# Shifted copies of y by quarter of the channels, the layer norm's steps in another order, and a second SiLU for the high part of z

## The chip, the cores and the metric

The kernel runs on one core of one Trainium2 chip. The metric is device time in microseconds (us) for one launch. The engines are named as the profile names them: PE (TensorE matmul) and PEld (its weight loads), DVE (VectorE), ACT (ScalarE), POOL (GpSimd), SP (SyncE, which issues nearly all DMAs here, in order).

## What is computed

A trunk of two layers works on 256 latent tokens and 256 context tokens of 1024 channels in float32. Layer 0 mixes tokens by a Conformer convolution module, layer 1 by retention, and each is followed by a SwiGLU network. Every sub-layer is an RMS norm with a shift, a scale and a gate that come from the condition (`adaln`). The change lies in the convolution module of layer 0, which runs on both sequences (512 tokens together):

```python
def conv_module(h, w1, b1, dw, dw_b, norm_g, w2):
    y = h @ w1 + b1
    a, gt = jnp.split(y, 2, axis=-1)
    y = a * jax.nn.sigmoid(gt)
    y = depthwise_conv(y, dw, width=31) + dw_b     # each channel by itself, along the tokens
    y = jax.nn.silu(layer_norm(y, norm_g))         # over the 1024 channels of a token
    return y @ w2

x = x + g_m * conv_module(modulate(x, norm_mix, sh_m, sc_m), ...)
x = x + g_f * swiglu_ffn(modulate(x, norm_ffn, sh_f, sc_f), ...)
```

The shifts, scales and gates are six vectors of 1024 for each sequence, `silu(c) @ ada_w + ada_b`. Three of them (mixer) are needed around the module, the FFN's shift and scale straight behind it.

## The kernel before

Channels lie on the 128 partitions, in eight blocks (`KC`), and the 512 tokens along the free dimension. Every large product is made of three matmuls (`mm3`) on values split into a rounded high part and a rest: high by high, high by low, low by high, in the type fp32r. The high part is a copy that rounds, the low part a subtraction.

The program is written in a layer that schedules by itself, with a timeline of its own, and sets the semaphores; instructions under `pin` keep the order in which they are written among the pinned ones of their engine. The products of w2 are not pinned, the ada blocks, the norm and the loads are.

For each block of channels the module forms a and g (`pair_half`, `start_products`), then y (`glu`), and the depthwise convolution's 31 taps are shared: 16 taps on PE (`dwconv_pe`), about nine on DVE (`dwconv_dve`), and five or six as ACT products with POOL additions (`dwconv_pool`). `total` adds the three. For PE's share, `bounce_out` writes y to DRAM (`yd`) and `bounce_in` reads it back into `z4`: four planes, one for each quarter of 32 channels, in which the 128 partitions hold the 32 channels of the quarter at four shifts of one token. One matmul (contraction over channel and shift, through the block-diagonal `dg`) then does four taps of 32 channels, and 16 of them make a block's `cv`. Before the change, SP issues `dg` and then four DMAs, one for each shift; each fills 32 partitions in all four planes. Blocks follow each other in a loop of eight steps; the convolution of block c stands two steps behind its y, and the last two blocks come after the loop.

The layer norm's mean and mean square come from matmuls: `stats(ch)` multiplies the block and its square by a column of 1/1024 (`mean32`) and adds up in the accumulator `pst` over all eight blocks. `pst` is copied to SBUF (`srow`), turned by a matmul (`ptk`, tokens on the partitions: tile `stats_t`) for the inverse root, which runs as thirteen small DVE steps on 128 x 4 values, and spread over all partitions for the mean (`mean_bc`, copy `mb`). POOL subtracts `mb` from the eight blocks; `token_row(rn)` spreads the inverse root (`rstd_bc`); then, block by block, DVE multiplies (`z_norm`, tile `zt`), ACT applies the SiLU with the gain (`zs`), DVE rounds the high part (`ah_z`) and subtracts for the low part (`al_z`), and PE multiplies by w2 (tile `w`, two halves n of the columns, four groups t of tokens, eight k).

Beside this, PE computes the vectors of `adaln`, in blocks i of 256 columns: `begin(i)` (16 matmuls, L239), `evict(i)` (ACT, L245), `cols(i)` (four small matmuls, L251) and `finish(i)` (ACT, L258). Blocks 8 to 11 are the mixer's gates, 12 to 19 the FFN's shift and scale. They serve as filling while the norm's chain runs: 8 to 15 stand before z, 16 and 17 in the z loop, 18 and 19 in the first half of w2. `gate_to_rows` turns the gates and sends them through DRAM. Blocks 12 to 15 are loaded into the memory of the module's input h (tags `ah` and `al`, which z takes over later), behind a small POOL memset; 16 and 17 into `z4`'s two buffers, 18 and 19 into others. PSUM has six accumulators (`acc`) and two `aux` tiles; `ADA_AUX` says which ada blocks use `aux`. Memory of the pool `cv` is given to later tiles (`crow`, `rawt`) when the z loop is done with it.

Of the kernel before, what the change touches and what calls it, by code (L numbers as in the profile page):

```python
# [8 lines left out]
F32 = mybir.dt.float32  # L9
F32R = mybir.dt.float32r  # L10
I32 = mybir.dt.int32
# [49 lines left out]
W2_AT = 3  # L61
PACC = 2
ADA_AUX = (16, 17, 18, 19)
ADA_K4 = (8, 9, 18)
# [17 lines left out]
def trunk_kernel(ctx: ExitStack, tc, x_in, ctx_in, cond, small, consts, rope, dist, ada, adas, adat,  # L82
# [406 lines left out]
    def bounce_in(ch, yd):  # L489

        n = GROUPS[ch]
        dg = cv.tile([P, MAXG, 4, 32], F32, tag="dg", name="dg", bufs=2)
        pin(nc.sync.dma_start(dg[:, :n], dwd[:, ch, :n]))
        z4 = cv.tile([P, 4, 2 * YW], F32, tag="z4", name="z4", bufs=Z4)
        w = 2 * YW - 3
        for s in range(4):
            pin(nc.sync.dma_start(z4[32 * s:32 * s + 32, :, 0:w], yd[:, :, s:s + w].rearrange("q c t -> c q t")))
        return z4, dg
# [67 lines left out]
    def stats(ch):  # L566
        for i, src in enumerate((yc[:, ch, :], sqs.pop(ch))):
            q = 2 * (ch % 2) + i
            pin(nc.tensor.matmul(pst[32 * q:32 * q + 32, :], mean32, src, start=(ch < 2), stop=(ch >= KC - 2)))
# [143 lines left out]
    fills = [pA.tile([P, 4096], F32, tag=tag, name=f"raw_fill_{tag}") for tag in ("ah", "al")]  # L713
    pin(nc.gpsimd.memset(fills[0][:, 0:1], 0.0))
    for i in range(12, 16):
        t = fills[(i - 12) // 2][:, 2048 * (i % 2):2048 * (i % 2) + 2048]
        pin(nc.sync.dma_start(t, ada[ADA_PE.index(i)]))
        ada_raws[i] = halves(t)
    w2r[0, 1] = load(w2[0, 1], name="w2_01", also=pin)
    for i in (16, 17):  # L720
        t = cv.tile([P, 4, 2 * YW], F32, tag="z4", name=f"raw_ada{i}", bufs=Z4).rearrange("p q t -> p (q t)")[:, 0:2048]
        pin(nc.sync.dma_start(t, ada[ADA_PE.index(i)]))
        ada_raws[i] = halves(t)
    cols(8)
# [10 lines left out]
    stats(c)  # L735
    cols(10)
    finish(10)
    begin(11)
    cbs[d] = dwconv_pe(d, zs4.pop(d))
    evict(11)  # L740
    cols(11)
    total(d)
    finish(11)
    square(d)
    stats(KC - 1)
    begin(12)
    srow = t2("srow")
    pin(nc.scalar.activation(srow, pst, AF.Copy))
    evict(12)
# [3 lines left out]
    pmd = aux("mean_bc")  # L753
    for q in range(4):
        pin(nc.tensor.matmul(pmd[32 * q:32 * q + 32, :], sel2[:, 0:1].to_broadcast([P, 32]), srow, start=True, stop=True))
    mb = cv.tile([P, 512], F32, tag="sq", name="mb", bufs=2)
    begin(13)
    cols(12)
    pin(nc.scalar.activation(mb, pmd, AF.Copy))
    evict(13)  # L760
    finish(12)
    cols(13)
    finish(13)
    gate_to_rows(0, 0, pin)
    gates = [gate_bc(0, 0, 0, pin), gate_bc(0, 0, 1, pin)]
    ada_raws[18] = ada_load(18, pin)
    ada_raws[19] = ada_load(19, pin)
    begin(14)
    evict(14)
    for ch in range(KC):  # L770
        pin(nc.gpsimd.tensor_tensor(yc[:, ch, :], yc[:, ch, :], mb, op=ALU.subtract))
    st = cv.tile([P, 4, 2], F32, name="st")
    nc.vector.tensor_copy(st.rearrange("p t i -> p (t i)"), ptk[:, 0:8])
    md, vv = st[:, :, 0], st[:, :, 1]
# [9 lines left out]
    mq = cv.tile([P, 4], F32, name="mq")  # L784
    va = cv.tile([P, 4], F32, name="va")
    rn = cv.tile([P, 4], F32, name="rn")
    nc.vector.tensor_tensor(mq, md, md, op=ALU.mult)
    nc.vector.scalar_tensor_tensor(va, vv, EPS, mq, op0=ALU.add, op1=ALU.subtract)

    nh, pt = ptk[:, 8:12], ptk[:, 12:16]  # L790
    nc.vector.tensor_scalar(rn.bitcast(I32), va.bitcast(I32), -0.5, 1597463007.0, op0=ALU.mult, op1=ALU.add)
    nc.vector.tensor_scalar(nh, va, -0.5, None, op0=ALU.mult)
    for i in range(3):
        nc.vector.tensor_tensor(pt, nh, rn, op=ALU.mult)
        nc.vector.tensor_tensor(pt, pt, rn, op=ALU.mult)
# [655 lines left out]
```

## Time and profile before

| what | value |
|---|---|
| median of three runs | 1101.52 us (1101.11 to 1102.01) |
| the profiled execution's own time | 1103.33 us |
| its span in the profile | 1101.2 us |
| mean granted PE clock | 0.991 |
| PE busy | 1069.0 us (97%) |
| DVE, ACT, POOL busy | 700.6, 417.5, 161.6 us |
| data moved | 190.29 MB, mean 173 GB/s |

The span is what the profile covers; the execution's own time has some 2 us around it. A busy PE is not PE at its peak: matmuls overlap, and their ends are modelled. A granted clock below 1.00 in a stretch means that PE ran its matmuls slower there. In a group's row, the name left of the arrow is the tile written; L507 and the like are lines of the kernel above.

### The profile page before, as it was taken

To read this page: it belongs to the slowest core of one execution; us is meant where nothing else is said; L and a number is where in the kernel's file an instruction comes from. 1 tells how busy PE (TensorE), PEld (TensorE's weight loads), DVE (VectorE), ACT (ScalarE), POOL (GpSimd) and SP (SyncE) were. 2 spreads that over 40 slices of the span, in tenths; PEclk is the share of its full clock that TensorE was granted. 3 is DMA by queue.
4 is the path that set the end of the run, shared out by engine and by line. 5 is a ranking of instruction groups with operands and counts; after the bars stand their busy time and mean duration, and the time that the engine had idled before them with its cause. 6 is when DMAs were issued, how large, how long until landed. Compare 5 with 4: busy or idle time off the path is not lost.

```text
span 1101.2 us, 13492 instructions
## 1 busy us (share of the span) xinstructions
PE 1069.0 (97%) x5302; PEld 845.0 (77%) x5302; DVE 700.6 (64%) x1147; ACT 417.5 (38%) x607; POOL 161.6 (15%) x119
## 2 busy tenths in 40 slices
PE   6989998999999999999999999999999989999998
PEld 2766654789888888888888788888888868888886
DVE  3988873757999877545644796366364555555445
ACT  4474463343222122212232564234333454444442
POOL 0077853030000000000000330000000461000000
PEclk8999998999999999999999999999999999999999
DMA  9469778732566576533313342334333344455551
GB/s 372 181 179 264 223 195 348 265 115 99 191 248 249 201 296 234 186 114 116 115 59 132 135 143 106 115 134 155 113 115 115 115 152 155 172 190 191 190 182 49
DMA packets 35185, 190.29 MB, mean 173 GB/s; under 512 B 3953, under 2 KB 4401, under 8 KB 16177
## 3 DMA queue, kind: packets, MB, share of 16 engines
q1 hardware_dynamic: 34688, 187.87, 49.0%
q10 hardware_dynamic: 434, 1.55, 0.4%
q8 instruction: 42, 0.69, 0.3%
q14 instruction: 21, 0.17, 0.0%
HBM read 185.99 MB, written 3.42 MB: 172 GB/s over the span
## 4 chain that ended last, share of the span: by engine, by line
PE 86%; DVE 6%; DMA 4%; ACT 3%; issue 1%; SPq 0%; POOL 0%; ACTq 0%; DVEq 0%
PE u L202 4%; PE fa L201 4%; PE u L200 4%; PE u L201 4%; PE fa L202 4%; PE fb L201 4%; PE fb L202 4%; PE fa L200 4%; PE fb L200 4%; PE v L201 3%; PE v L202 3%; PE v L200 3%; PE dn L201 3%; PE dn L202 3%; PE dn L200 3%; PE cv L507 2%
## 5 line engine op out<-in xcount | busy, mean ns | idle before, releaser
L171 DVE TENSOR_TENSOR wl_gu<-raw_gu,wh_gu 128x1024 fp32r<-128x1024 f32 x76 | 92.2, 1223 | 82.6 <-ACT wh_gu L163 81.7
L163 ACT ACTIVATE wh_gu<-raw_gu 128x1024 fp32r<-128x1024 f32 x84 | 88.0, 1058 | 139.6 <-PE fb L201 52.6
L851 DVE SCALAR_TENSOR_TENSOR junk<-raw_adat,crow 128x1024 f32<-128x1024 f32 x80 | 97.5, 1219 | 0.9
L171 DVE TENSOR_TENSOR wl_dn<-raw_dn,wh_dn 128x1024 fp32r<-128x1024 f32 x38 | 46.5, 1224 | 45.3 <-ACT wh_dn L163 45.0
L200 PE MATMUL fa<-ah_h0f,wh_gu 128*128 128x512 f32 (+1 forms) x192 | 72.0, 376 | 1.0 <-DVE ah_h0f L324 1.0
L201 PE MATMUL fa<-al_h0f,wh_gu 128*128 128x512 f32 (+1 forms) x192 | 72.3, 376 | 0.1
L200 PE MATMUL fb<-ah_h0f,wh_gu 128*128 128x512 f32 (+1 forms) x192 | 72.1, 376 | 0.0
L202 PE MATMUL fa<-ah_h0f,wl_gu 128*128 128x512 f32 (+1 forms) x192 | 72.0, 375 | 0.0
L202 PE MATMUL fb<-ah_h0f,wl_gu 128*128 128x512 f32 (+1 forms) x192 | 72.0, 375 | 0.0
L201 PE MATMUL fb<-al_h0f,wh_gu 128*128 128x512 f32 (+1 forms) x192 | 72.0, 375 | 0.0
L163 ACT ACTIVATE wh_dn<-raw_dn 128x1024 fp32r<-128x1024 f32 x38 | 40.3, 1060 | 80.1 <-PE dn L202 35.5
L200 PE MATMUL u<-wh_gu,ah_h1f 128*128 128x512 f32 x160 | 63.5, 397 | 0.0
L171 POOL TENSOR_TENSOR wl_qk<-raw_qk,wh_qk 128x1024 fp32r<-128x1024 f32 x4 | 9.6, 2401 | 362.8 <-DVE res L355 350.3
L202 PE MATMUL u<-wh_gu,al_h1f 128*128 128x512 f32 x160 | 62.8, 393 | 0.0
L201 PE MATMUL u<-wl_gu,ah_h1f 128*128 128x512 f32 x160 | 62.2, 390 | 0.0
L523 POOL TENSOR_TENSOR pacc<-pacc,pr 128x512 f32<-128x512 f32 x39 | 58.8, 1508 | 17.8 <-ACT pr L522 15.5
L540 DVE SCALAR_TENSOR_TENSOR lacc<-y,sm,lacc 128x512 f32<-128x512 f32 x65 | 49.1, 755 | 2.1
L201 PE MATMUL v<-wl_v,ah_h 128*128 128x512 f32 x128 | 50.4, 393 | 0.0
L202 PE MATMUL v<-wh_v,al_h 128*128 128x512 f32 x128 | 50.1, 391 | 0.0
L200 PE MATMUL dn<-wh_dn,ah_hid 128*128 128x512 f32 x128 | 49.9, 390 | 0.0
L201 PE MATMUL dn<-wl_dn,ah_hid 128*128 128x512 f32 x128 | 49.8, 389 | 0.0
L202 PE MATMUL dn<-wh_dn,al_hid 128*128 128x512 f32 x128 | 49.8, 389 | 0.0
(308 smaller groups left out, 2669.5 us busy)
## 6 DMA issues: line engine op xcount, KB each, us to landing
raw_gu<-in_gu_dram SPq DMA_DIRECT2D x44, 1024.0 KB, 4.8
raw_adat<-in_adat_dram SPq DMA_DIRECT2D x28, 1024.0 KB, 4.9
raw_dn<-in_dn_dram SPq DMA_DIRECT2D x19, 1024.0 KB, 4.8
raw_ada<-in_ada_dram SPq DMA_DIRECT2D x10, 1024.0 KB, 10.8
z<-yd SPq DMA_DIRECT2D x32, 284.5 KB, 4.9
raw_qk<-in_wqk_dram SPq DMA_DIRECT2D x8, 1024.0 KB, 4.7
raw_v<-in_wv_dram SPq DMA_DIRECT2D x8, 1024.0 KB, 4.8
raw_g<-in_wg_dram SPq DMA_DIRECT2D x8, 1024.0 KB, 4.8
```

The lines of the kernel that those rows point to most:

```text
L163: also(nc.scalar.activation(hi[:, :m], raw[:, c:c + m], AF.Copy))
L171: also((eng or nc.vector).tensor_tensor(lo[:, :m], raw[:, c:c + m], hi[:, :m].bitcast(F32), op=ALU.subtract))
L200: also(nc.tensor.matmul(o, a[0], b[0], start=first, stop=False))
L201: also(nc.tensor.matmul(o, a[0], b[1], start=False, stop=False))
L202: also(nc.tensor.matmul(o, a[1], b[0], start=False, stop=last))
L507: pin(nc.tensor.matmul(cb[32 * q:32 * q + 32, :], dg[:, g, q, :], m, start=(g == 0), stop=(g == n - 1)))
L523: pin(nc.gpsimd.tensor_tensor(pacc, pacc, pr, op=ALU.add))
L540: pin(nc.vector.scalar_tensor_tensor(cacc, a, w, cacc, op0=ALU.mult, op1=ALU.add))
L851: pin(nc.vector.scalar_tensor_tensor(junk, raw[:, c, :], 1.0, crow[:, s, :], op0=ALU.mult, op1=ALU.mult, accum_out=mods[l][:, c0 + c, s:s ...
```

## The change

`bounce_in` issues one DMA for each quarter: its source pattern has 32 channels, four shifts of one token and the row, so that each DMA fills one plane on all 128 partitions, now in the order channel, shift (the host lays out `dwd` to match). The DMAs of z4 come before that of `dg`.

In the norm, the sums in `pst` end with the seventh block; `srow` and its transpose no longer hold the eighth. The eighth block and its square are multiplied as stationary operands with one column of `mean32`, which gives sums for each token on the partitions, and DVE adds both (once to SBUF, once to PSUM). The mean is spread by `token_row`, like the inverse root. The small DVE steps work on PSUM columns. All of these are pinned.

The ada blocks are placed anew: 8 to 10 before the last convolution, 11 and 12 and the sums of 13 between there and z, the rest of 13, and 14 and 15, in the z loop, 16 to 19 in the first half of w2. Their loads move: 12 and 13 into `ah` (without the memset), 14 and 15 into `z4`, 18 and 19 into a pool that opens after the z loop. In the z loop, ACT writes z's high part by a SiLU of its own and runs a second one into PSUM, from which the low part is formed.

```diff
@@ -59,9 +59,11 @@
 K4 = 5
 YW = TOK + 2 * PAD
 W2_AT = 3
+W2_ADA = (2, 4, 6, 7)
 PACC = 2
-ADA_AUX = (16, 17, 18, 19)
-ADA_K4 = (8, 9, 18)
+ADA_AUX = (14, 15, 16, 17, 18, 19)
+ADA_K4 = (8, 9, 16)
+ADA_RAWT = (18, 19)
 T2 = 5
 GU_POOL = (0, 1)
 CTX_AT = ((1, 3), (1, 4), (1, 6), (1, 7))
@@ -489,12 +491,13 @@
     def bounce_in(ch, yd):
         n = GROUPS[ch]
+        z4 = cv.tile([P, 4, 2 * YW], F32, tag="z4", name="z4", bufs=Z4)
+        w = 2 * YW - 3
+        for q in range(4):
+            src = yd[q]
+            pin(nc.sync.dma_start(z4[:, q, 0:w], bass.AP(src.tensor, src.offset, [[2 * YW, 32], [1, 4], [1, w]])))
         dg = cv.tile([P, MAXG, 4, 32], F32, tag="dg", name="dg", bufs=2)
         pin(nc.sync.dma_start(dg[:, :n], dwd[:, ch, :n]))
-        z4 = cv.tile([P, 4, 2 * YW], F32, tag="z4", name="z4", bufs=Z4)
-        w = 2 * YW - 3
-        for s in range(4):
-            pin(nc.sync.dma_start(z4[32 * s:32 * s + 32, :, 0:w], yd[:, :, s:s + w].rearrange("q c t -> c q t")))
         return z4, dg
     def dwconv_pe(ch, zd):
@@ -566,7 +569,7 @@
     def stats(ch):
         for i, src in enumerate((yc[:, ch, :], sqs.pop(ch))):
             q = 2 * (ch % 2) + i
-            pin(nc.tensor.matmul(pst[32 * q:32 * q + 32, :], mean32, src, start=(ch < 2), stop=(ch >= KC - 2)))
+            pin(nc.tensor.matmul(pst[32 * q:32 * q + 32, :], mean32, src, start=(ch < 2), stop=(ch >= KC - 3)))
     ys, zs4, cbs = {}, {}, {}
@@ -710,17 +713,19 @@
     total(c)
     dve_taps(d, cut, TAPS)
-    fills = [pA.tile([P, 4096], F32, tag=tag, name=f"raw_fill_{tag}") for tag in ("ah", "al")]
-    pin(nc.gpsimd.memset(fills[0][:, 0:1], 0.0))
-    for i in range(12, 16):
-        t = fills[(i - 12) // 2][:, 2048 * (i % 2):2048 * (i % 2) + 2048]
+    fill = pA.tile([P, 4096], F32, tag="ah", name="raw_fill")
+    for i in (12, 13):
+        t = fill[:, 2048 * (i % 2):2048 * (i % 2) + 2048]
         pin(nc.sync.dma_start(t, ada[ADA_PE.index(i)]))
         ada_raws[i] = halves(t)
-    w2r[0, 1] = load(w2[0, 1], name="w2_01", also=pin)
-    for i in (16, 17):
+    def load_z4(i):
         t = cv.tile([P, 4, 2 * YW], F32, tag="z4", name=f"raw_ada{i}", bufs=Z4).rearrange("p q t -> p (q t)")[:, 0:2048]
         pin(nc.sync.dma_start(t, ada[ADA_PE.index(i)]))
         ada_raws[i] = halves(t)
+    load_z4(14)
+    w2r[0, 1] = load(w2[0, 1], name="w2_01", also=pin)
     cols(8)
     finish(8)
     begin(9)
@@ -733,45 +738,31 @@
     finish(9)
     evict(10)
     stats(c)
+    srow = t2("srow")
+    pin(nc.scalar.activation(srow, pst, AF.Copy))
     cols(10)
     finish(10)
-    begin(11)
     cbs[d] = dwconv_pe(d, zs4.pop(d))
-    evict(11)
-    cols(11)
+    load_z4(15)
+    ada_raws[16] = ada_load(16, pin)
+    ada_raws[17] = ada_load(17, pin)
     total(d)
-    finish(11)
     square(d)
-    stats(KC - 1)
-    begin(12)
-    srow = t2("srow")
-    pin(nc.scalar.activation(srow, pst, AF.Copy))
-    evict(12)
     ptk = aux("stats_t")
     for t in range(4):
         pin(nc.tensor.matmul(ptk[:, 2 * t:2 * t + 2], srow[:, P * t:P * t + P], sel2, start=True, stop=True))
-    pmd = aux("mean_bc")
-    for q in range(4):
-        pin(nc.tensor.matmul(pmd[32 * q:32 * q + 32, :], sel2[:, 0:1].to_broadcast([P, 32]), srow, start=True, stop=True))
-    mb = cv.tile([P, 512], F32, tag="sq", name="mb", bufs=2)
-    begin(13)
-    cols(12)
-    pin(nc.scalar.activation(mb, pmd, AF.Copy))
-    evict(13)
-    finish(12)
-    cols(13)
-    finish(13)
-    gate_to_rows(0, 0, pin)
-    gates = [gate_bc(0, 0, 0, pin), gate_bc(0, 0, 1, pin)]
-    ada_raws[18] = ada_load(18, pin)
-    ada_raws[19] = ada_load(19, pin)
-    begin(14)
-    evict(14)
-    for ch in range(KC):
-        pin(nc.gpsimd.tensor_tensor(yc[:, ch, :], yc[:, ch, :], mb, op=ALU.subtract))
-    st = cv.tile([P, 4, 2], F32, name="st")
-    nc.vector.tensor_copy(st.rearrange("p t i -> p (t i)"), ptk[:, 0:8])
-    md, vv = st[:, :, 0], st[:, :, 1]
+    st = cv.tile([P, 2, 8], F32, name="st")
+    pin(nc.vector.tensor_copy(st[:, 0, :], ptk[:, 0:8]))
+    for i, src in enumerate((yc[:, d, :], sqs.pop(d))):
+        for t in range(4):
+            pin(nc.tensor.matmul(ptk[:, 16 + 2 * t + i:17 + 2 * t + i], src[:, P * t:P * t + P], mean32[:, 0:1],
+                                 start=True, stop=True))
+    pin(nc.vector.tensor_tensor(st[:, 1, :], ptk[:, 16:24], st[:, 0, :], op=ALU.add))
+    pin(nc.vector.tensor_tensor(ptk[:, 24:32], ptk[:, 16:24], st[:, 0, :], op=ALU.add))
+    md, vv = (st[:, 1, :].rearrange("p (t i) -> p t i", i=2)[:, :, i] for i in range(2))
+    mdp = ptk[:, 24:32].rearrange("p (t i) -> p t i", i=2)[:, :, 0]
     def token_row(cols, name):
@@ -781,26 +772,31 @@
                                  start=True, stop=True))
         return pb
-    mq = cv.tile([P, 4], F32, name="mq")
-    va = cv.tile([P, 4], F32, name="va")
+    pmd = token_row(md, "mean_bc")
+    mb = cv.tile([P, 512], F32, tag="sq", name="mb", bufs=2)
+    pin(nc.scalar.activation(mb, pmd, AF.Copy))
+    begin(11)
+    evict(11)
+    for ch in range(KC):
+        pin(nc.gpsimd.tensor_tensor(yc[:, ch, :], yc[:, ch, :], mb, op=ALU.subtract))
     rn = cv.tile([P, 4], F32, name="rn")
-    nc.vector.tensor_tensor(mq, md, md, op=ALU.mult)
-    nc.vector.scalar_tensor_tensor(va, vv, EPS, mq, op0=ALU.add, op1=ALU.subtract)
-    nh, pt = ptk[:, 8:12], ptk[:, 12:16]
-    nc.vector.tensor_scalar(rn.bitcast(I32), va.bitcast(I32), -0.5, 1597463007.0, op0=ALU.mult, op1=ALU.add)
-    nc.vector.tensor_scalar(nh, va, -0.5, None, op0=ALU.mult)
+    mq, va, nh, pt = (ptk[:, c:c + 4] for c in (32, 36, 8, 12))
+    pin(nc.vector.tensor_tensor(mq, mdp, md, op=ALU.mult))
+    pin(nc.vector.scalar_tensor_tensor(va, vv, EPS, mq, op0=ALU.add, op1=ALU.subtract))
+    pin(nc.vector.tensor_scalar(rn.bitcast(I32), va.bitcast(I32), -0.5, 1597463007.0, op0=ALU.mult, op1=ALU.add))
+    pin(nc.vector.tensor_scalar(nh, va, -0.5, None, op0=ALU.mult))
     for i in range(3):
-        nc.vector.tensor_tensor(pt, nh, rn, op=ALU.mult)
-        nc.vector.tensor_tensor(pt, pt, rn, op=ALU.mult)
-        nc.vector.scalar_tensor_tensor(rn, pt, 1.5, rn, op0=ALU.add, op1=ALU.mult)
+        pin(nc.vector.tensor_tensor(pt, nh, rn, op=ALU.mult))
+        pin(nc.vector.tensor_tensor(pt, pt, rn, op=ALU.mult))
+        pin(nc.vector.scalar_tensor_tensor(rn, pt, 1.5, rn, op0=ALU.add, op1=ALU.mult))
+    cols(11)
+    finish(11)
+    begin(12)
+    evict(12)
     prs = token_row(rn, "rstd_bc")
-    cols(14)
-    finish(14)
-    begin(15)
-    evict(15)
-    cols(15)
-    finish(15)
+    cols(12)
+    begin(13)
     z = new_act(pA, "z")
     zts = {}
@@ -816,22 +812,35 @@
         if ch + 1 < KC:
             z_norm(ch + 1)
         zs = pz[ch % 2]
+        pin(nc.scalar.activation(z[0][:, ch, :], zts[ch], AF.Silu, scale=cn[:, ch:ch + 1]))
         pin(nc.scalar.activation(zs, zts[ch], AF.Silu, scale=cn[:, ch:ch + 1]))
-        split_to(z[0][:, ch, :], z[1][:, ch, :], zs, pin)
+        pin(nc.vector.tensor_tensor(z[1][:, ch, :], zs, z[0][:, ch, :].bitcast(F32), op=ALU.subtract))
         if ch == W2_AT:
             split_w2(0, 1, None, pin)
+        if ch == 0:
+            finish(12)
+            evict(13)
+        if ch == 1:
+            cols(13)
+            finish(13)
+            gate_to_rows(0, 0, pin)
+            gates = [gate_bc(0, 0, 0, pin), gate_bc(0, 0, 1, pin)]
         if ch in (2, 4):
-            begin(15 + ch // 2)
-            evict(15 + ch // 2)
+            begin(13 + ch // 2)
+            evict(13 + ch // 2)
         if ch in (3, 5):
-            cols(15 + ch // 2)
-            finish(15 + ch // 2)
+            cols(13 + ch // 2)
+            finish(13 + ch // 2)
     cvs.close()
     pB = ctx.enter_context(tc.tile_pool(name="pB", bufs=1))
-    for i in range(2):
-        w2r[1, i] = load(w2[1, i], name=f"w2_1{i}", also=pin)
     ads = ExitStack()
     ad = ads.enter_context(tc.tile_pool(name="ad", bufs=1))
+    w2r[1, 0] = load(w2[1, 0], name="w2_10", also=pin)
+    for i in ADA_RAWT:
+        t = ad.tile([P, 2048], F32, tag="rawt", name=f"raw_ada{i}", bufs=2)
+        pin(nc.sync.dma_start(t, ada[ADA_PE.index(i)]))
+        ada_raws[i] = halves(t)
+    w2r[1, 1] = load(w2[1, 1], name="w2_11", also=pin)
     crow = ad.tile([P, 2, D], F32, name="crow")
     for s in range(2):
@@ -874,12 +883,16 @@
             mm3(pw[t], (z[0][:, k, tk], z[1][:, k, tk]), w(k), k == 0, k == KC - 1, last)
             if k == KC - 1:
                 residual(t, n, pw[t], gates[t // 2], last)
-            if not n and t == 3 and k in (3, 5):
-                begin(18 + k // 5)
-                evict(18 + k // 5)
-            if not n and t == 3 and k in (4, 6):
-                cols(18 + k // 6)
-                finish(18 + k // 6)
+            if not n and t == 3 and k in W2_ADA:
+                i = 16 + W2_ADA.index(k)
+                if i > 16:
+                    cols(i - 1)
+                    finish(i - 1)
+                begin(i)
+                evict(i)
+            if n and (t, k) == (0, 0):
+                cols(19)
+                finish(19)
             if n and (t, k) == (1, KC - 1):
                 mod_scale(0, 1)
                 h = new_act(pB, "h0f")
@@ -1397,10 +1410,10 @@
     w1b = np.ascontiguousarray(w1[:, :, :, K_PAIRS:].transpose(3, 1, 0, 2, 4)).reshape(KC - K_PAIRS, P, 2048)
-    dwd = np.zeros((4, 32, KC, MAXG, 4, 32), f32)
+    dwd = np.zeros((32, 4, KC, MAXG, 4, 32), f32)
     dwt = i["conv_dw"][0][:4 * MAXG].reshape(MAXG, 4, KC, 4, 32)
     for c in range(32):
-        dwd[:, c, :, :, :, c] = dwt[:, :, :, :, c].transpose(1, 2, 0, 3)
+        dwd[c, :, :, :, :, c] = dwt[:, :, :, :, c].transpose(1, 2, 0, 3)
     dwd = dwd.reshape(P, KC, MAXG, 4, 32)
     def nblk(w, kb, n):
```

## The prediction

> **What bounds the kernel now.** I read the page first: what is busy, and which engine the chain that ended last runs through.
>
> ```profile
> span 1101.2 us, 13492 instructions
> PE 1069.0 (97%) x5302; PEld 845.0 (77%) x5302; DVE 700.6 (64%) x1147; ACT 417.5 (38%) x607; POOL 161.6 (15%) x119
> PE 86%; DVE 6%; DMA 4%; ACT 3%; issue 1%; SPq 0%; POOL 0%; ACTq 0%; DVEq 0%
> ```
>
> TensorE (PE) is the bound nearly everywhere. A change outside its arithmetic pays only where PE idles or runs at a low clock, so I looked for such stretches near the edited lines: the chain in order of time from 150 to 190 us (start, length, what; the longest pieces).
>
> ```profile
> 158.20 7.58 DMA z<-yd
> 165.92 5.37 PE cv L507 x32
> 171.31 0.70 DVE yc L630
> 172.06 1.24 PE stats L569 x3
> ...
> 174.72 0.98 PE stats_t L752 x8
> ...
> 179.62 1.00 PE ada L239 x16
> 180.62 1.09 PE rstd_bc L780 x8
> ...
> 183.18 0.39 ACT adasb L245
> 183.62 0.62 PE ada L251 x4
> 184.26 0.41 ACT mods L258 x2
> 184.68 0.59 ACT zs L819
> 185.29 0.70 DVE ah_z L324
> 186.03 0.50 PE w L200
> ```
>
> The last channel block's shifted copies land at 165.8; its convolution (cv) ends at 171.3; the layer norm takes until 186.03, when the second pointwise product (w) gets its first z. Then the windows: busy time per engine, PE clock, DMA share, GB/s.
>
> ```profile
> 158.00:164.00 6.00, 5.85 (x70) 2.92 (x70) 5.65 (x9) 2.42 (x9) 4.34 (x5) 1.00 1.02 211
> 164.00:166.00 2.00, 0.29 (x8) 0.11 (x8) 0.25 (x1) 0.39 (x1) 0.00 (x0) 1.00 0.78 306
> 166.00:170.00 4.00, 4.00 (x24) 1.32 (x27) 0.00 (x0) 0.00 (x0) 0.00 (x0) 0.57 1.01 424
> 171.00:186.00 15.00, 11.76 (x117) 7.15 (x113) 4.91 (x18) 6.89 (x21) 8.55 (x7) 1.00 0.79 317
> 186.00:190.00 4.00, 3.96 (x16) 2.48 (x20) 3.86 (x7) 0.69 (x1) 1.32 (x2) 0.58 0.99 328
> 190.00:216.00 26.00, 26.00 (x161) 19.72 (x154) 18.26 (x25) 12.28 (x20) 0.00 (x0) 1.00 0.72 256
> 174.00:179.00 5.00, 4.71 (x44) 2.82 (x42) 2.24 (x14) 2.50 (x8) 1.55 (x2) 1.00 1.02 424
> ```
>
> PE idles 2 - 0.29 = 1.7 us before cv and 15 - 11.76 = 3.2 us in the norm, and after each gap it works at a clock of 0.57 to 0.58 for 4 us, which loses 4 x 0.43 = 1.7 us each time: 8.3 us in all. That is the whole prize. From 190 on PE is full (26.00 of 26), so every piece of PE work pushed behind the first w product costs its full length.
>
> **The change part by part.**
>
> *A, the shifted copies.* The same bytes move (4 x 284.5 KB a block), but each DMA now fills one quarter's plane on all 128 partitions instead of four planes on 32.
>
> ```profile
> 156.89 1.74 SPq L497 DMA_DIRECT2D z<-yd  x4
> z<-yd SPq DMA_DIRECT2D x8, 284.5 KB, 5.6
> dg<-in_dwd_dram SPq DMA_DIRECT2D x2, 256.0 KB, 3.2
> 162.60 0.61 PE L251 MATMUL ada<-cst,adasb 128*128 128x2 f32 x4
> 143.95 3.62 PE L507 MATMUL cv<-z,dg 128*32 128x512 f32 x32
> ```
>
> At 158 to 164 the queues are full (share 1.02) and yet move 211 GB/s, with almost only these copies in flight; at 166 to 170 the large loads reach 424 GB/s at the same share. So the copies run at half rate. The rate of the new ones lies between 211 and 424; I take the upper end, since the loads, too, write all 128 partitions. Then 1.17 MB (four times 284.5 KB) needs 2.8 us instead of 5.5, and the last copy lands near 162. dg, formerly issued ahead, in SyncE's wait for yd, now comes last: issue at 158.6, plus 3.2 is 161.9. Neither is late: PE has the columns of ada block 10 until 163.2 (162.60 + 0.61), and block 11 no longer stands between. So cv starts at 163.2 instead of 165.92, without the gap before it, at full clock (3.62 instead of 5.37), and ends near 166.85: 4.45 us early. [...]
>
> On SyncE the fill loads of blocks 12 and 13 no longer wait for a memset behind POOL's taps, and start about 159; those of 15, 16 and 17 wait for cv's end. None is used before it has had several us, so I cost this at nothing. For the seven earlier blocks A is free as well: the only waits of PE there hang on DVE and ACT.
>
> ```profile
> 82.58 3.64 PE L507 MATMUL cv<-z,dg 128*32 128x512 f32 x32 [1.32 <-ACT pr L522]
> ```
>
> If that 1.32 us were the copies after all, it would be a gain on top.
>
> *B, the norm.* Before, cv's end to the first w is 186.03 - 171.3 = 14.7 us. After, by the rows above and these:
>
> ```profile
> 172.13 0.63 ACT L564 ACTIVATE sq<-yc 128x512 f32<-128x512 f32 x1
> 176.14 0.16 DVE L788 SCALAR_TENSOR_TENSOR va<-st,mq 128x4 f32<-128x4 f32 x1
> 184.56 1.30 ACT L819 ACTIVATE zs<-zt,sm 128x512 f32<-128x512 f32 x2
> ```
>
> The transpose of the seven-block sums (0.98) comes first, under the last add of yc; then 4 matmuls on yc and 4 on sq. No row has a one-column matmul with yc as the stationary side; the nearest is stats_t, four such in 0.98 with two columns, so 0.98 for each four (from half of that to the 1.09 of rstd_bc). The square (0.63) is done by then. 166.85 + 3 x 0.98 = 169.8; DVE add 0.2, 170.0; mean_bc as a token row 1.09, 171.1; block 11: sums 1.00, eviction 0.39 in the open, columns 0.62, 173.2; block 12's sums 1.00, 174.2; rstd_bc 1.09, 175.3; columns of 12, sums of 13, 176.9. Hidden: the copy mb and POOL's subtractions beside block 11, the thirteen small DVE steps at about 0.2 with the handover (0.16 in the row) beside 11 and 12, and zt beside 13. If block 12 were gone, about nothing of the DVE steps would show. z's high part lies where blocks 12 and 13 were loaded, so its SiLU waits for 13's sums: 0.65 plus handovers, first w near 177.65. That is 10.8 us after cv, 3.9 less than before; the cast (0.70) left the path, and the chain no longer waits for block 15's eviction, columns and mods. With A the first w comes 186.03 - 177.65 = 8.4 us early.
>
> *C, PE work that moves behind the first w.* Before, blocks 16 to 19 stand there; after, 14 to 19 and the columns of 13: 2 x (1.00 + 0.62) + 0.62 = 3.9 us, on a full PE: +3.9.
>
> *D, the low clock at 186 to 190.* It followed 3 us of near-idle PE; now the longest gap is z's 0.75 us. The clock stays up: -1.7 (bounds 0 and -1.7).
>
> *E, the z loop.* The second SiLU adds 8 x 0.65 = 5.2 us to ACT; DVE loses eight casts of 0.70. The low part is ready no earlier than before, the high part one cast sooner. PE takes 12 matmuls a channel:
>
> ```profile
> 213.15 0.39 PE L201 MATMUL w<-wl_w,ah_z 128*128 128x512 f32 x1
> 217.46 0.39 PE L202 MATMUL w<-wh_w,al_z 128*128 128x512 f32 x1
> ACT mods L258 <- PE ada L251: 10.9, 7, 7.1
> 203.97 0.80 SPq L838 DMA_DIRECT2D crow<-in_cond_dram  x2
> ```
>
> These are 20 in a row, 0.227 apart, so 2.7 us a channel against 1.3 on ACT: z is not the bound. Two things can leave PE short. Blocks 12 and 13 now hold accumulators (six in all, two for zs) until their mods are written, so two of w's four tiles are free at the start and the rest 1 to 3 us later; bounds 0 and 2 us, I take +0.7. And the loads of 18 and 19, with w2's last part behind them, go where crow went, into memory that the last zt releases. crow's DMA starts 17.9 us after the first w; as late after it, they start at 195.6, and at 424 GB/s (2.5 us each) 18 is in by about 199, all three by 204. PE asks for 18 at the seventh channel, 177.65 + 6 x 2.7 + 7.1 for the columns of 13 and blocks 14 to 17 = 201: hidden, barely.
>
> Sum: -8.4 + 3.9 - 1.7 + 0.7 = -5.5 us. The other way round: 8.3 us lost, less what stays open (0.2 + 0.45 + 0.75), less E's 0.7, less new work on PE (1.96 for the eight matmuls and 0.1 for the token row, less about 0.9 for the last stats, whose 1.24 holds a wait) leaves 5.0. I take 5.3. The profiled execution took 1103.33 us with a span of 1101.2; the median of the runs is 1101.52, 1.8 lower, and the difference is applied to it: 1096.2.
>
> **The rivals.**
>
> 1. *The copies are no faster* (the change doesn't do what it says). The 2.3 KB pieces, not the partitions, set the rate. dg then comes last, cv starts at 166.3 after a gap, at the low clock, and ends at 171.7. -3.5 (B less 0.4) + 3.9 - 1.7 + 0.7 = -0.6: 1100.9. For it: dg, in 2 KB pieces on all partitions, took 3.2 us for 256 KB, no hurry either; against it: that is the latency of a lone transfer, while four copies in a full queue stay at 211 GB/s.
> 2. *The clock falls in the norm.* From 166.85 to 169.8 PE runs only one- and two-column matmuls. [...] One spell costs 1.7 us as the two seen: 1097.9.
> 3. *Round trips through ACT (slower).* In the z loop ACT waits for PE at seven places (13's eviction and mods, the two gate copies, 14's and 15's). Where PE has run dry meanwhile, each costs an eviction, a SiLU and handovers, 0.39 + 0.65 + 0.1 = 1.15 us. It takes five in the open to eat 5.3; with all seven, -5.3 + 8 is 1104.2. For it: ACT waited 10.9 us on columns. Against: PE was never idle in that time (26.00 of 26).
> 4. *The early copies count too*: 1.32 more at 82 us, 1094.9.
>
> **How the numbers follow.** About 0.2% (2.2 us) is what a measurement of this kernel can tell from no change. Forecast 0.57, rival 1 0.13, rival 2 0.15, rival 3 0.07, rival 4 0.08. Faster: forecast, 2 and 4, 0.80; same: rival 1, 0.13; slower 0.07. The forecast's own range is 1094.5 to 1098 (E's 0 to 2, C and B's small steps). The stated range, 1094.0 to 1101.0, takes in rivals 1, 2 and 4 and leaves out rival 3 and the tails.
>
> **What the profile after would show.** Copies landing about 3.5 us after issue with over 350 GB/s in the queues; cv of the last block without idle time before it and in 3.6 us; about 11 us from its end to the first w product; a clock of 1.00 from 150 to 216; six ada blocks behind the first w, and PE full until the residual of the first tile. I am wrong if cv still waits for a DMA, if the clock falls around 170, or if PE idles between w products behind SiLU, accumulators or the load of block 18.

## The result, and the profile after

The changed kernel is slower by 1.1%: 1114.39 us (1110.96 to 1115.75, four runs) against 1101.76 us (1101.11 to 1103.97, four runs), a ratio of 1.0109 (95% interval 1.0093 to 1.0126). 1096.2 was forecast. The page of the changed kernel first, profiled in an execution of 1113.95 us.

```profile
span 1112.2 us, 13507 instructions
PE 1075.9 (97%) x5314; PEld 850.1 (76%) x5314; DVE 697.2 (63%) x1141; ACT 422.4 (38%) x615; POOL 161.4 (15%) x118
```

The span grew by 11.0 us and PE's busy time by 6.9, though it counts only twelve matmuls more: much of it is the same work at a lower clock. The chain shows where (start, length, what).

```profile
159.23 5.64 DMA dg<-in_dwd_dram
...
165.00 6.47 PE cv L510 x32
171.47 1.00 PE stats_t L754 x8
...
172.72 2.29 PE stats_t L759 x16
...
175.26 2.08 PE mean_bc L771 x8
177.33 1.91 PE ada L241 x16
...
182.58 2.00 PE rstd_bc L771 x8
...
186.75 0.50 PE w L202
```

The last convolution waits for dg and ends at 171.47, where it ended before (171.29). The last copy had landed only 0.7 us before dg, at 164.2 (issued at 158.6, 5.6 us to landing). The norm takes 15.3 us from the end of cv, not 10.8; an ada block of 1.00 us takes 1.9, `mean_bc` and `rstd_bc` 2.0 to 2.1 each where 1.09 was forecast. In the windows the clock is the third column from the right.

```profile
158.00:164.00 6.00, 5.14 (x55) 2.59 (x54) 5.65 (x9) 2.92 (x10) 4.38 (x4) 0.99 0.89 272
164.00:166.00 2.00, 1.00 (x8) 0.40 (x12) 0.33 (x1) 0.00 (x0) 0.00 (x0) 0.50 0.99 406
166.00:170.00 4.00, 4.00 (x24) 0.96 (x20) 0.00 (x0) 0.00 (x0) 0.00 (x0) 0.50 1.01 426
...
175.00:185.00 10.00, 9.24 (x60) 6.36 (x64) 2.66 (x16) 1.78 (x5) 6.89 (x6) 0.53 0.64 259
186.00:190.00 4.00, 3.25 (x16) 2.71 (x17) 2.18 (x4) 3.51 (x10) 1.99 (x2) 1.00 0.01 2
190.00:216.00 26.00, 26.00 (x152) 19.43 (x151) 14.28 (x20) 14.03 (x25) 0.00 (x0) 1.00 0.64 228
```

At 175 to 185 PE is busy for 9.24 of 10 us, and yet the clock is at half. At 190 to 216 PE is full and at full clock, as forecast. The second loss lies behind that. First ACT's instructions in order of time there, then the chain, then the wait of the next norm's transpose (us in total, how often, the longest).

```profile
214.75 2.01 ACT L165 ACTIVATE wh_w<-raw_w 128x1024 fp32r<-128x1024 f32 x2 [5.36 <-DMA raw_w<-in_w_dram]
216.89 2.26 ACT L848 ACTIVATE crow<-crow 128x1024 f32<-128x1024 f32 x2
219.06 0.37 ACT L247 ACTIVATE adasb<-ada 128x256 f32<-128x256 f32 x1
```

```profile
226.15 0.34 PE ada L253 x4
...
238.26 0.62 PE ada L253 x4
```

```profile
PE tr L344 <- DVE xn L314: 5.8, 1, 5.8
```

The eviction of ada block 16 stands on ACT behind a split of w2's last part, which waits 5.36 us for its load, and behind crow's SiLU. Its columns then run on PE only at 226.15, those of block 19 at 238.26. The FFN's shift and scale are late, and the FFN's norm, formerly beside the last products, lies bare: PE waits 5.8 us.

The kernel before was profiled once more (run before_again, below); that execution took 1099.95 us. Four windows of it, and then of the changed kernel:

```profile
153.00:187.00 34.00, 29.70 (x287) 15.11 (x289) 19.05 (x39) 13.93 (x38) 16.30 (x14) 0.97 0.81 286
187.00:213.00 26.00, 26.00 (x159) 19.48 (x152) 18.30 (x25) 11.79 (x20) 0.00 (x0) 0.98 0.76 286
213.00:240.00 27.00, 25.70 (x131) 21.37 (x130) 15.00 (x36) 10.99 (x20) 7.07 (x3) 1.00 0.39 150
240.00:272.00 32.00, 31.27 (x233) 29.16 (x232) 23.21 (x45) 13.19 (x22) 2.41 (x1) 1.00 0.32 116
```

```profile
153.00:187.00 34.00, 30.27 (x235) 15.98 (x234) 15.27 (x34) 9.90 (x24) 15.28 (x13) 0.75 0.69 268
187.00:213.00 26.00, 26.00 (x153) 19.41 (x153) 13.74 (x18) 15.29 (x32) 0.99 (x1) 1.00 0.52 192
213.00:240.00 27.00, 25.30 (x154) 19.78 (x152) 10.49 (x15) 9.90 (x19) 3.86 (x2) 1.00 0.61 215
240.00:272.00 32.00, 26.56 (x195) 24.78 (x196) 22.17 (x56) 15.12 (x27) 5.61 (x3) 0.89 0.25 91
```

I count as lost the idle time (length less PE's busy time) and busy time x (1 - clock). Before: 4.3 + 0.9, 0.5, 1.3, 0.7, together 7.7 us. After: 3.7 + 7.6, 0, 1.7, 5.4 + 2.9, together 21.3. The difference of 13.6 is most of the 14.4 us between the two spans. About 6 of it is lost up to the first w, 8 in the tail at 213 to 272.

### The profile page after: what moved, and what is told of

Same layout as the page of the kernel before. It is cut to its first block, busy times and chain, and to the rows that moved or that the text cites. A ratio compares the mean times of both kernels' runs of the same rounds, so it can differ in the third digit from the quotient of the medians.

```text
span 1112.2 us, 13507 instructions
## 1 busy us (share of the span) xinstructions
PE 1075.9 (97%) x5314; PEld 850.1 (76%) x5314; DVE 697.2 (63%) x1141; ACT 422.4 (38%) x615; POOL 161.4 (15%) x118
## 4 chain that ended last, share of the span: by engine, by line
PE 86%; DVE 6%; ACT 3%; DMA 3%; issue 1%; SPq 0%; POOL 0%; ACTq 0%; DVEq 0%
PE u L204 4%; PE u L202 4%; PE u L203 4%; PE fa L203 4%; PE fa L204 4%; PE fa L202 4%; PE fb L203 4%; PE fb L204 4%; PE fb L202 4%; PE v L203 3%; PE v L204 3%; PE v L202 3%; PE dn L202 3%; PE dn L203 3%; PE dn L204 3%; PE cv L510 2%
```

## The experiments

### Up to the norm: dg, the copies, the fills

**dg_first.** The changed kernel with dg issued ahead of the copies.

```diff
 def bounce_in(ch, yd):
+    dg = cv.tile(...); pin(nc.sync.dma_start(dg[:, :n], dwd[:, ch, :n]))
     z4 = ...            # the four quarter copies
-    dg = cv.tile(...); pin(nc.sync.dma_start(dg[:, :n], dwd[:, ch, :n]))
```

> The changed kernel with dg issued ahead of the four copies again. If dg's place alone held up the last convolution (it waited 1.7 us, until dg landed at 164.9), the convolution starts at 163.2 without a gap, the clock stays up, and the norm runs at full clock: some 7 us less, about 1107. If the copies themselves land at about 164.2 (last issue 158.6 and up to 5.6 us), the gap shrinks by less than 1 us, the clock falls as before, and the time stays at 1112 to 1115.

1107.24 us (1106.52 to 1108.07), ratio 1.0055 (1.0038 to 1.0072): 6 to 7 us of the loss go with this one line. Its chain, and its windows:

```profile
157.78 6.37 DMA z<-yd
...
164.19 4.35 PE cv L510 x28
...
180.94 0.50 PE w L202
```

```profile
153.00:187.00 34.00, 31.60 (x261) 18.70 (x253) 17.39 (x38) 12.99 (x34) 16.31 (x13) 0.95 0.72 268
...
213.00:240.00 27.00, 20.54 (x133) 15.78 (x131) 10.08 (x26) 7.38 (x19) 4.67 (x2) 0.93 0.58 205
```

cv runs at full clock and the first w comes 5.8 us earlier. Up to 187 it now loses 2.4 + 1.6 us, less than the kernel before; the tail keeps its loss (6.5 + 1.4 at 213 to 240). The last copy is no earlier for it: it lands at 164.9 (issued at 158.4, 6.5 us to landing), inside cv. What the line saves is mostly clock; tail_fix, below, shows one execution with dg late and the clock up.

**old_copies.** The changed kernel with `bounce_in` and the host's layout as before (four planes to 32 partitions each, dg first).

> The changed kernel with the shifted copies and dg as they were before (four planes to 32 partitions each, dg issued first); all the rest of the change stays. Theory (with dg last, the new copies gained nothing at the last block: cv ended at 171.47 against 171.29): as the changed kernel, 1113 to 1116, and dg first is worth about 7 us only together with the new copies. Rival (the new copies gain in the seven earlier blocks too, or shorten the wait of the last): 1117 or more.

1110.99 us (1107.33 to 1114.93), ratio 1.0090 (1.0061 to 1.0119). Not above the changed kernel, so the new copies with dg behind them bring nothing over the old ones with dg ahead; the median lies under the 1113 to 1116 that I expected, and the intervals overlap.

**fills_late.** The changed kernel, dg last, with one line put back, so that the fill loads of blocks 12 and 13 wait for GpSimd's taps again.

```diff
     fill = pA.tile([P, 4096], F32, tag="ah", name="raw_fill")
+    pin(nc.gpsimd.memset(fill[:, 0:1], 0.0))
```

> The changed kernel (dg still last) with one line put back: a memset on GpSimd into the tile of the fill loads of ada blocks 12 and 13, so that SyncE issues these 2 MB only behind GpSimd's taps, as before, not right behind the copies and dg. Theory (the early fills share the DMA engines with dg and the last copies; dg took 5.6 us against 3.2): dg lands in 3.2 to 4 us, by 163.5, cv starts at about 163.5 with little gap at full clock, first w near 181: 1107 to 1109, as dg_first (1107.2). Rival (dg is late because it is issued behind four issues of 0.6 us and lands late whatever follows it): cv still at 165, 1113 to 1116.

1112.19 us (1108.58 to 1116.3), ratio 1.0084 (1.0056 to 1.0112), and dg is as late as it was:

```profile
159.80 6.07 DMA dg<-in_dwd_dram
```

My theory fell: the early fills are not what delays dg. What is left is the four copies ahead of it on the same queue: over all eight blocks dg takes 4.8 to 6.1 us behind them in the changed kernel (median 5.5), and 3.4 in the median ahead of them in the kernel before.

**quarter_alone.** The kernel before with the quarter copies alone, dg first.

> The kernel before with the copies by quarter alone (dg first, all else as before). If the copies to all partitions run faster and arrive some 1.5 to 2.5 us earlier, the last convolution starts earlier by that: 1 to 4 us less than before (the upper end if the clock stays up), 1098 to 1100.5. If they are no faster, 1101.5 to 1102; if their dearer issue (0.6 instead of 0.43 us each) eats the gain, the same.

1100.77 us (1098.03 to 1102.18), ratio 0.9995 (0.9984 to 1.0007).

```profile
163.96 3.62 PE cv L508 x32
```

```profile
159.00:160.00 1.00, 1.00 (x16) 0.39 (x12) 1.00 (x2) 0.12 (x1) 0.92 (x2) 1.00 1.03 357
...
162.00:163.00 1.00, 1.00 (x10) 0.64 (x12) 0.96 (x2) 0.17 (x2) 0.31 (x2) 1.00 0.13 46
```

cv does not wait, but the gain is too small to measure. The windows show the copies by themselves, since no other load is issued until 162.34. From 158 to 163 the queues move 1.16 MB, just these four copies. They reach 357 GB/s where the queues are full, against 194 to 232 before (159 to 163, by the same windows), and by 162 to 163 they are nearly idle. Yet the last copy counts as landed only at 163.9 (issued at 158.5, 5.4 us to landing). **before_again**, the kernel before once more, tells what else was missing:

> The kernel before, unchanged, for a second profile. Theory (the profiled execution of before, 1103.33 us at a mean clock of 0.991, had spells of low clock that its usual execution, near 1101 at 0.996, does not have, so the prediction counted on a gain from clock that was not there): at least one of the two spells at 166 to 170 and 186 to 190 is missing. Rival (both spells belong to the kernel): both are there, and the difference lies elsewhere.

```profile
158.25 6.70 DMA z<-yd
165.08 3.67 PE cv L507 x32
...
183.50 0.50 PE w L200
```

The windows after cv's start and after the first w:

```profile
166.00:170.00 4.00, 3.74 (x34) 1.38 (x26) 0.69 (x1) 0.70 (x3) 0.00 (x0) 1.00 1.01 420
186.00:190.00 4.00, 4.00 (x25) 2.35 (x25) 3.46 (x7) 1.86 (x4) 0.00 (x0) 0.71 0.97 328
```

In this execution cv is at full clock though it waits for the copies; the low clock at 166 to 170, on which the forecast counted, is not there, and at 186 to 190 it was 0.71 instead of 0.58. The first w comes at 183.5, not 186.03. Against this the quarter copies save 1.1 us before cv, not 4.45 (their last copy lands at 163.9, that of before_again at 164.95). Both are single executions; of the 29 of the kernel before that ran beside silu_alone the mean clock has a median of 0.997, and only four lie at 0.991 or 0.992, as the first profile does.

### The clock in the norm

**dense** puts seven dense 512-column matmuls (results unused) on PE ahead of the last cv, into the wait for dg; **dense_mid** adds four more ahead of `mean_bc`.

```diff
+    dense(7)
     cbs[d] = dwconv_pe(d, zs4.pop(d))
...
+    dense(4)                                  # dense_mid only
     pmd = token_row(md, "mean_bc")
```

> The changed kernel with seven dense matmuls (128x128 by 512, operands at hand, result unused) on PE ahead of the last convolution, in the time in which it waits for its data anyway. Theory: PE's idle 1.7 us drop the clock there, and the low clock carries on into the norm; kept busy, the convolution takes 3.65 us instead of 6.47 and the norm some 11 us instead of 15.3: 6 to 7 us less, about 1107. Rival: the clock falls in the norm by itself, because its one- and two-column matmuls do not keep it up; then only the convolution gains, 2.8 us, about 1111, with a clock of 0.5 somewhere between 170 and 185.

> The changed kernel with seven dense 512-column matmuls ahead of the last cv, as in the run called dense, and four more between the one- and two-column matmuls and mean_bc; their results are not used. Theory (the tiny matmuls of the norm are what drops the clock, though PE is busy): the clock stays up at 172 to 182, where dense lost 4.7 us; less about 1 us of added PE work that is 3.7 below dense: about 1107. Rival (the clock falls because PE waits for ACT and DVE, or from load before, whatever PE is given there): low clock again at 172 to 182, 1110.5 to 1112.

dense: 1110.76 us (1108.91 to 1111.35), ratio 1.0087 (1.0072 to 1.0102). dense_mid: 1107.73 us (1107.17 to 1109.79), ratio 1.0063 (1.0048 to 1.0078). The window from 153 to 187 of dense, then of dense_mid:

```profile
153.00:187.00 34.00, 31.74 (x255) 18.74 (x254) 17.03 (x37) 12.25 (x32) 16.27 (x13) 0.85 0.69 268
```

```profile
153.00:187.00 34.00, 32.25 (x278) 19.63 (x276) 18.74 (x39) 13.31 (x36) 16.34 (x13) 1.00 0.69 268
```

With cv kept at full clock the clock still fell in the norm (31.74 x 0.15 = 4.8 us lost); with four dense matmuls behind the tiny ones it stayed up. The intervals of the two ratios overlap a little. Nor is it shown that the dense matmuls did it: in the profile of mended_mid, below, the clock fell in spite of them (0.73 at 174 to 179), and in that of tail_fix it held without them.

### Behind the z loop

**tail_fix.** The changed kernel (dg last) with w2's last part loaded ahead of 18 and 19, the first product of n = 1 pinned, and the two splits pinned behind the evictions of 17 and 19.

```diff
+    w2r[1, 1] = load(...)                     # behind w2r[1, 0], ahead of blocks 18 and 19
-            last = pin if n and t > 1 else ...
+            last = pin if n and (t > 1 or (t, k) == (0, 0)) else ...
                 evict(i)
+                if k == 4: split_w2(1, 0, None, pin)
+                if k == 7: split_w2(1, 1, None, pin)
```

> The changed kernel with the second half of w2 held behind ada block 19's sums, w2's last part loaded ahead of blocks 18 and 19, and its split on ACT behind their evictions. Theory: the FFN's norm lay bare (PE idle 5.8 us, then 2.2 us lost to the low clock) because the last four ada blocks came too late in the order; then these 7 us go, less up to 2.4 us of waits for ACT between the blocks: 1108 to 1110. Rival: the loads of 18 and 19, which wait for the last zt, are what is late; then PE waits for them in the first half of w2 and the time stays at 1113 to 1115.

1112.67 us (1109.79 to 1124.29), ratio 1.0127 (1.0070 to 1.0184): no gain. ACT now waits for crow's DMA ahead of the same eviction, which runs at 211.97:

```profile
ACT crow L848 <- DMA crow<-in_cond_dram: 7.1, 1, 7.1
```

The profile also bears on the clock. PE waits for dg as in the changed kernel, the norm is the same and holds no dense matmuls, and yet the clock is at 1.00 throughout:

```profile
167.39 3.64 PE cv L510 x32
...
182.02 0.50 PE w L202
```

```profile
153.00:187.00 34.00, 30.31 (x269) 18.50 (x268) 20.23 (x41) 14.28 (x35) 16.34 (x13) 1.00 0.69 268
```

So neither the wait for dg nor the tiny matmuls lower the clock in every execution. In most it does fall there: of the ten kernels here with the new norm and no dense matmuls inside it, nine were profiled with a clock of 0.60 to 0.86 between cv's end and the first w, all but this one. In the six profiles with the old norm it was 1.00 there; in one of them (the second run of quarter_silu, 0.95 at 153 to 187) it fell just before the first w, while PE waited for z.

**mended** is dg_first with tail_fix's repairs, and crow's SiLU pinned behind block 19 as well.

> The changed kernel with dg issued ahead of the copies and four repairs of the order behind the z loop: w2's last part loaded ahead of blocks 18 and 19, its two splits behind the evictions of blocks 17 and 19, the first product of n = 1 pinned behind block 18, crow's SiLU behind block 19. Theory (late dg and the ada chain behind w2's split are the two causes of the loss): dg first alone gave 1107.2; the lost time of PE at 213 to 272 in the changed kernel was 9.4 us against 2.0 before, so 7.4 more go: 1099 to 1101, with the norm of the next layer hidden and PE idle under 2 us at 213 to 272. Rival (the stall behind the z loop only moves to the next thing in ACT's order, as in tail_fix): 1104 to 1108, with a gap of PE over 2 us between 190 and 272.

1101.25 us (1098.51 to 1105.95), ratio 1.0004 (0.9988 to 1.0020): the whole loss is gone, and no more. Two kernels tell its repairs apart: **dg_w2** has dg first and only the earlier load, **dg_order** has all of mended but the earlier load.

> The kernel of dg_first (the changed one with dg ahead of the copies), and w2's last part loaded ahead of ada blocks 18 and 19; the order of ACT and PE is left as it is. Theory A (the step that failed is the time of the load: the eviction of block 16 waits behind the split of w2's last part, which waits for its load): the load comes 2 to 5 us earlier and the bare norm of the next layer shrinks with it: 1101 to 1104, against 1107.2. Theory B (it is the order on ACT: the eviction of block 16 stands behind three things that come late, the last of them crow's SiLU, so an earlier load only changes which of them it waits for): 1105.5 to 1108.

> The kernel called mended without its earlier load of w2's last part: dg ahead of the copies, the two splits of w2's last parts pinned behind the evictions of blocks 17 and 19, the first product of n = 1 behind block 18, crow's SiLU behind block 19; the loads in the changed kernel's order. Theory A (the time of the load decides): the tail stays, 1105 or more. Theory B (the order on ACT and PE decides): as mended, 1100 to 1102.5, with PE idle under 2 us at 240 to 272.

dg_w2: 1108.32 us (1106.97 to 1110.97), ratio 1.0065 (1.0046 to 1.0083). dg_order: 1101.74 us (1100.28 to 1106.05), ratio 1.0008 (0.9996 to 1.0020). So it is the order, not the load. In dg_w2, ACT evicts block 16 at 211.90, and PE turns to its columns 10 us later (ACT's rows, the chain):

```profile
211.90 0.36 ACT L247 ACTIVATE adasb<-ada 128x256 f32<-128x256 f32 x1
```

```profile
221.87 0.34 PE ada L253 x4
```

On PE the unpinned products of n = 1 stand in between; I suppose that in the scheduler's own timeline the eviction comes late, but no run shows that timeline. In dg_order, with block 16's sums at nearly the same time (202.4 against 202.2), ACT evicts it at 203.6 and its columns run at 208.4. dg_order changes the order on ACT and on PE at once, and no run parts the two fully; tail_fix, with PE's order pinned and crow's SiLU left ahead of the eviction, gained nothing. In dg_order the window from 240 to 272 is as before the change:

```profile
240.00:272.00 32.00, 31.32 (x240) 29.48 (x239) 22.37 (x44) 14.84 (x24) 3.58 (x2) 1.00 0.32 118
```

### Versions of it

**mended_mid** is mended with four dense matmuls ahead of `mean_bc`; **mended_late** is mended with the memset of fills_late.

> The kernel called mended, with four dense 512-column matmuls ahead of mean_bc (results not used). Theory (in dg_first the clock fell once in the norm and lost 1.65 us; four dense matmuls of about 0.25 us hold it): 0.5 to 1 us below mended, near 1099. Rival (the clock does not fall there once dg is in time, or falls regardless): 0.5 to 1 us above mended.

> The kernel called mended (dg first, the order behind the z loop repaired) with the same memset line put back. Theory (the fills also slow the copies: with dg first the last copy landed at 164.2, 6.4 us after its issue): cv starts at 163.5 without a gap, 0.7 us earlier, and the idle time in front of it, which ages the clock, is gone: 1099 to 1100.5, 0.5 to 2 us under mended. Rival (no effect beside the scatter of the clock, or blocks 12 and 13 come too late): 1101 to 1103.

mended_mid: 1101.38 us (1099.67 to 1104.62), ratio 1.0003 (0.9991 to 1.0015), no different from mended, whose own executions spread widely (the profiled one took 1104.70 us, with a clock of 0.85 at 153 to 187). mended_late: 1101.34 us (1099.31 to 1103.1), ratio 0.9990 (0.9978 to 1.0003). Its cv, its first w and its clock:

```profile
163.14 4.31 PE cv L510 x32
...
179.92 0.50 PE w L202
```

```profile
153.00:187.00 34.00, 31.98 (x278) 19.11 (x277) 17.80 (x39) 13.87 (x35) 16.38 (x14) 0.95 0.71 268
```

**silu_alone** is the kernel before with the second SiLU alone, **quarter_silu** with the quarter copies (dg first) and the second SiLU, run twice.

> The kernel before with the high part of z by a second SiLU alone; copies, norm and loads as before. Theory (the cast of 0.70 us, less the longer way of the high part through ACT, leaves the path of the first w): 1100.5 to 1101, 0.3 to 0.8 us under before. Rival (it is what made quarter_silu 2 to 3 us faster, quarter copies alone being no faster): 1098.5 to 1099.8. Other rival (ACT's work delays the ada evictions): 1101.5 or more.

> The kernel before with two parts of the change alone: the quarter copies (dg still first) and the high part of z by a second SiLU; the order of the norm, of the ada blocks and of the loads is that of before. Theory (the cast of 0.7 us leaves the path of the first w and the clock stays up): first w 0.6 us earlier than with the quarter copies alone (182.3 there), 1099.5 to 1100.5. Rival (ACT's second SiLU of 0.65 us delays the evictions of the ada blocks in the z loop, and w waits): 1101 or more.

> The kernel of quarter_silu once more, beside silu_alone on one chip, since 0.3% is near what a comparison can tell. Theory (it is faster than before): ratio 0.9960 to 0.9985, and below silu_alone. Rival (the first comparison was luck of the clock): 0.9985 to 1.0005.

silu_alone: 1099.68 us (1097.53 to 1103.09), ratio 0.9986 (0.9973 to 1.0000). quarter_silu: 1099.28 us (1097.01 to 1101.76), ratio 0.9971 (0.9959 to 0.9983), and again 1098.86 us (1097.56 to 1101.96), ratio 0.9981 (0.9971 to 0.9991). This version beats both kernels, by 2 to 3 us. PE's wait for z's high part, in the group of w's first product of before_again and then of silu_alone (last column: idle before it), accounts for 0.7 us of it; the rest is not traced.

```profile
L200 PE MATMUL w<-wh_w,ah_z 128*128 128x512 f32 x64 | 26.0, 408 | 1.8 <-DVE ah_z L324 1.8
```

```profile
L200 PE MATMUL w<-wh_w,ah_z 128*128 128x512 f32 x64 | 25.6, 402 | 1.1 <-ACT ah_z L819 1.1
```

## Why the prediction was wrong, step by step

The forecast missed by 18.2 us (1114.39 against 1096.2). About 7 of them go with dg's place (dg_first, 1107.24), and 6 more with the order behind the z loop (mended, 1101.25). The last 5 are a gain that was not there: in mended_late the first w comes 3.6 us before that of before_again, not 8.4 us early.

**The prize.** 8.3 us was read from one execution of 1103.33 us. Some 3.4 of it was low clock. By the same count before_again lost 5.2 + 0.5 us at 153 to 213, and cv's low clock was not among it. The step that failed is taking the clock of one execution for the kernel's.

**A, the copies: failed at "Neither is late".** Both were. dg was forecast to land 3.2 us after an issue at 158.6; it was issued at 159.23, since the four issues took 0.60 us each and not 0.43, and took 5.64. The 3.2 was the price of dg with no copies ahead of it. The last copy was forecast near 162; it landed at 164.2 in the changed kernel and, with dg first, at 163.9 in quarter_alone and 164.9 in dg_first. The rate was not what failed: by the windows of quarter_alone the bytes were through near 162. What the forecast left out is the time from the last bytes to the landing, some 1.7 us there by an estimate from those rows (163.9 less 162.2). Rival 1 thus had the wrong cause, for the copies were faster, and in pieces of 2.3 KB as before; its effect, a cv that starts late behind dg and at a low clock, came true. The forecast took 424 GB/s for them, twice the old rate; the runs show 357 against 194 to 232 GB/s, which is 1.5 to 1.8 times, not quite two. Why they are faster is not shown. That each fills all 128 partitions was the author's reason for the upper end; but the four old copies fill all four ranges of 32 partitions and are under way together (in the kernel before the first lands at 160.5, the last is issued at 158.2), so that together they too cover all partitions.

**B, the norm: right in its shape, wrong in its clock.** In tail_fix, at full clock, it takes 182.02 - 171.03 = 11.0 us from cv's end to the first w, against 10.8 forecast. In mended_late it takes 179.92 - 167.45 = 12.5, and PE lost 31.98 x 0.05 = 1.6 us of clock up to the first w. In the changed kernel the clock lost 7.6 us at 153 to 187, part of it in cv behind the wait for dg, where rival 2 had one spell of 1.7. Rival 2 named what most profiles show, nine of ten; its term was mis-sized, because a spell was priced by the two of 4 us seen, while this one lasted some 10 us (0.53 over 175 to 185). Why the clock falls in one execution and not in another stays open.

**C** was right: from the first w to 240 us the ada blocks take 9.8 us of PE in mended_late and 6.9 in before_again, of which 0.9 is low clock (1.87 us for a block of 1.00), so 3.8 more against 3.9 forecast. It takes back the 3.6 us by which the first w is earlier, and mended_late is hardly faster than the kernel before. **D** was right behind the first w (1.00 at 186 to 190, where before_again has a spell of low clock from about 184.9 to 188.3 that loses 1.7 us); but about as much is lost again in the new norm.

**E, the z loop.** The accumulators cost nothing, where 0.7 was forecast: the 0.75 us idle at 186 to 190 lie before the first w at 186.75, where PE waits for z's high part, and from there PE is full. What failed is "hidden, barely". I followed the loads of 18, 19 and w2's last part only up to PE's demand. The load of w2's last part was late for its split on ACT, behind which block 16's eviction was queued; but dg_w2 shows that an earlier load does not help. It is the order: what stands ahead of the eviction on ACT, and the unpinned products of n = 1 that the scheduler puts on PE between an eviction and its columns. The forecast looked at neither order. Worth 8 us in the changed kernel, by the windows at 213 to 272; 1107.24 against 1101.74 by dg_first and dg_order.

**Rivals 3 and 4.** PE was full at 190 to 216, so the round trips in the z loop cost nothing: the slower case was priced at the wrong place. Rival 4 brought nothing either. In the changed kernel the wait for pr at 82 us is 2.2 us, not less than the 1.32 seen before. In quarter_alone it is gone, with 0.8 us of waiting for copies in its place; but the next block's cv starts only 0.25 us earlier (97.93 against 98.18), and in silu_alone, with the old copies, as early (97.99).

## What to carry to other kernels

Before a gain is counted in clock, see whether a second execution has the same spell. A transfer moved behind others on its queue (dg here: 5.5 us in the median, 3.4 before) is priced with that queue full, up to its landing and not to its last bytes, and if the bound engine needs it, it goes first. Where work is moved into a stretch that a scheduler orders by itself, follow the moved instruction on every engine that it passes, to the last thing that needs its result; here the load that looked late was not the cause, and the order on ACT and PE was.

## What the hardware showed

In the changed kernel the clock fell at 174 to 175 (1.00 at 173 to 174, 0.58 there), while PE ran one- and two-column matmuls almost without a gap (busy for 3.27 us from 171.47 to 175.0, the rows of `stats_t` in the chain), and it stayed near half until about 184.5 (0.53 at 175 to 185), though PE was busy for 9.24 of those 10 us. In tail_fix the same matmuls ran and it stayed at 1.00. What sets the clock is not shown by these runs. Four dense matmuls are not shown to hold the clock (1.00 in dense_mid, 0.73 at 174 to 179 in mended_mid).

Filling 128 partitions with one issue (one row on each) took SyncE 0.60 us here where 32 (four rows on each) took 0.43, for the same bytes. The rows of the changed kernel and of the kernel before, with the shortest, median and longest issue in ns:

```profile
L498 SPq DMA_DIRECT2D z<-yd x4: 525/596/602, 156.7 to 158.6; - x4
```

```profile
L497 SPq DMA_DIRECT2D z<-yd x4: 318/427/430, 156.9 to 158.2; - x4
```
